# A mixture-of-experts kernel whose last block becomes a pair of experts, with a down projection in a half and two quarters of the columns

## The chip, the cores and the metric

One Trainium2 chip; the program runs on one core. The metric is the device time of one execution in microseconds (us). Three timed executions of the kernel before gave 731.32, 733.75 and 733.29 us, a median of 733.29.

## The reference

The input is 512 tokens of width 1024. One layer is computed: a mixer (two parallel groups of heads with a common input and output projection), then a mixture of experts, then a final RMSNorm. The change lies wholly in the mixture of experts and the norm:

```python
y = (silu(xb @ w1[e]) * (xb @ w3[e])) @ w2[e]      # one expert, 1024 -> 512 -> 1024, float32
out[token] += weight * y                            # two experts for each token
x = x + g2 * out
return x * rsqrt(mean(x * x) + 1e-6) * final_g
```

There are 32 experts; each has three matrices of 2 MB, so the experts' weights are some 200 MB, and each byte is read once.

## The kernel before, in words

The first part of the span (up to about 235 us) is the mixer, the router and the sorting of experts by the number of their tokens. The rest is 13 blocks (`BLOCKS`, line 30). A block takes 128 slots, which two experts share with 64 slots each (a pair) or four experts with 32 each (a quad). Ten blocks are pairs, three are quads. The order of the blocks is written out in line 30; the last one (number 12) is the quad `QUADS[2]`, and before it come four pairs.

**One block** (`block`, line 1075) does the following on TensorE, in an order written by hand (line 1280). `up` (line 1100) multiplies the gathered tokens by w1: eight steps of k, in each one product of 512 columns for each expert, and each product lies in its own strip of 32 or 64 of the array's columns. A SiLU goes to ScalarE, some small products and transposes follow (lines 1118 to 1125), then `up` with w3, the gating product on VectorE (line 1131), four transposes and a copy (`hidden_t`, line 971), and the down projection `mm` (line 1146): for each of four chunks q of the hidden width, for each half of the output columns, for each expert one product. In all blocks but the last, `expert_out` (line 979) then multiplies by the gate `g2b`, splits the result into a high and a low half (`split`, line 85: a copy on ScalarE, a subtraction on VectorE), and returns eight units of `combine_units` (line 955). A unit is two products that bring the 128 slots back to 128 tokens, for one half of the columns, and an addition to `x2` on VectorE. The units are run in the next block, between its other products; blocks 10 and 11 also gather the tokens of block 12.

**The last two blocks** differ. Block 12 has no tokens to gather for anyone, so `block` gets the eight units of block 11 as `along`, and runs one of them behind each of the eight steps of its w1 (line 1106). Ahead of it, once block 11 is done, lines 1301 to 1309 spread `final_g` over the partitions with copies on VectorE and products on TensorE.

**The weights** come by DMAs of the SP queue in the order in which the blocks need them (line 1093): w1, w3, w2 of a block, then the next block. They go through a ring of 12 buffers of 8 KB a partition (`RING`, line 38). One buffer is filled by two DMAs of 512 KB, one for each of two experts; a buffer is loaded again when TensorE has read it. The program gives eight semaphores in turn to the DMAs, so that a DMA is issued when the eighth one before it has landed. A row of a DMA is 4 KB long for w1, w3 and w2, except for the last block's w2, which is loaded by columns.

**The end.** `LAST` (line 42) cuts the last block's down projection into four parts of 256 columns, each with its own weights (rows of 1 KB). `y_part` (line 1320) runs the 16 products of a part (four chunks, four experts; the trace lists every such product twice), then the multiplication by `g2b` (line 1327) and, except in the last part, the split. `combine_part` (line 1337) brings a part back to the four groups of 128 tokens: products (line 1344), the addition on VectorE (line 1346), a sum of squares on ScalarE (line 1348); in the first two parts GpSimd multiplies by `fg` (line 1350). In the last part ScalarE also takes the square roots (line 1354). Lines 1371 to 1378 set the order: parts 0 and 1, combine 0, part 2, combine 1, part 3, combine 2, combine 3. In this stretch (line 1313) the order of every engine is the order of the program. `scales` and `finish` then scale the rows and send them out.

Of the kernel before, what the change touches and what calls it, by code (L numbers as in the profile page):

```python
# [12 lines left out]
OP = mybir.AluOpType  # L13
# [5 lines left out]
E, F, FC = 32, 512, 4  # L19
SLOT = 64  # L20
FIXED = 4
# [5 lines left out]

PAIRS = [(FIXED + 2 + i, 2) for i in range(0, MID, 2)]
QUADS = [(FIXED + 2 + MID + i, 4) for i in range(0, SMALL, 4)]
BLOCKS = [(0, 2), (2, 2), QUADS[0], PAIRS[0], (FIXED, 2), PAIRS[1], PAIRS[2], QUADS[1], *PAIRS[3:], QUADS[2]]  # L30
NB = len(BLOCKS)
FB, FA = 4, 3
F0 = 8
# [5 lines left out]
FIRST = ["wp"] * WP + ["wq"] * WQ + ["ft"] * 4 + ["l8"] * 3  # L39
WARM = 18  # L40
EPS = 1e-6
LAST = tuple((slice(c, c + 256), 4) for c in range(0, 1024, 256))


@with_exitstack
def trunk(ctx, tc, a, out):
    nc = tc.nc
    sync, act, pool, dve, pe = nc.sync, nc.scalar, nc.gpsimd, nc.vector, nc.tensor
# [15 lines left out]
    def bank(tag=None, shape=(P, 512), dt=F32):  # L64
        if tag is None:
            tag = ring[turn[0] % 3]
            turn[0] += 1
        return psum.tile(list(shape), dt, name=tag)
# [10 lines left out]
    def t2(shape):  # L79
        return ft.tile(list(shape), F32, name="t2", bufs=6)  # L80
# [98 lines left out]
    class Ada:  # L179
# [19 lines left out]
        def mm(self, kk=None):  # L199
            if kk != 1:  # L200
                self.ps = bank("m")
            for k in range(KD) if kk is None else range(4 * kk, 4 * kk + 4):
                j = k % 4
                pe.matmul(self.ps[32 * j:32 * j + 32], cond[:, k:k + 1].to_broadcast([P, 32]), self.w[k // 4][:, j, :],  # L204
                          start=(k < 4), stop=(k >= 4), tile_position=(0, 32 * j))
            if kk != 0:
                self.m = t2((P, 512))
                act.activation(self.m, self.ps, AF.Copy)
# [336 lines left out]
    for k in range(KD):  # L545
# [9 lines left out]
        if k == 4:  # L555
# [5 lines left out]
            for c in range(4):  # L561
                dve.scalar_tensor_tensor(sbb[:, c, :], pt[:, c, :], cb_("lnb", c), sbb[:, c, :], op0=OP.mult,
                                         op1=OP.add)
# [84 lines left out]
    for c in range(4):  # L648
# [3 lines left out]
        for t in range(NT):  # L652
            for h in range(2):
# [6 lines left out]
                                 op0=OP.mult, op1=OP.add)  # L660
# [369 lines left out]
    class Weights:  # L1030
# [3 lines left out]
        def __init__(self, name, b, f, cs=None, n=1):  # L1034
            if b not in experts:
                experts[b] = []
                for e in range(BLOCKS[b][0], BLOCKS[b][0] + BLOCKS[b][1]):
                    if e >= FIXED:
# [21 lines left out]
    def block_weights(b):  # L1060
        if b == NB - 1:
            w2 = [Weights("expert_w2", b, D, cs, n) for cs, n in LAST]
        else:
# [3 lines left out]
    def columns(b):  # L1067

        if BLOCKS[b][1] == 4:
            return [(32 * j, 32, j) for j in range(4)]  # L1070
        if BLOCKS[b][0] == FIXED:
            return [(32 * j, 32, j // 3) for j in range(4)]
        return [(64 * j, 64, j) for j in range(2)]

    def block(b, along, early, before_y, after):

        last = b == NB - 1
        p0, np_ = BLOCKS[b]
        cols = columns(b)
        w1, w3, w2 = block_weights(b) if b != 1 else second  # L1080
        if b == 0:
            slots.extend(FIRST)
            w3.load()
            w1.load(1)
            for w in w2:
                w.load()
            second.extend(block_weights(1))
            second[0].load(2)
            w1.load()
            xT4b.append(const.tile([P, KD, 4 * SLOT], F32, name="l8", bufs=5))  # L1090
            kept.append(const.tile([P, 2, D], F32R, name="l8", bufs=5))
        else:
            for w in [w1, w3] + w2:
                w.load()
        w1, w3, w2 = w1.r, w3.r, [w.r for w in w2]
        yb = kept[0]
        sl = slice((b % 2) * P, (b % 2 + 1) * P)
        g, xT = g4s[b // 2][:, :, sl], xT4b[b // 2 % 2][:, :, sl]

        def up(w, units=()):  # L1100
            h = bank("h")
            for k in range(KD):
                for c, n, j in cols:
                    pe.matmul(h[c:c + n], xT[:, k, c:c + n], w[j][k],  # L1104
                              start=(k == 0), stop=(k == KD - 1), tile_position=(0, c))
                for u in units[k:k + 1]:
                    u()
            return h

        if b == 0:  # L1110
            h3 = up(w3)
        h1 = up(w1, along)
        s = t2((P, F))
        act.activation(s, h1, AF.Silu)  # L1114
        if last:
            act.activation(over_i, s[:, 0:1], AF.Sqrt, scale=0.0, bias=eps)
        ps = bank("m", (P, 2, np_))
        for t in range(NT):
            pe.matmul(ps, g[:, t, :], wtp[:, t, :, p0:p0 + np_], start=(t == 0), stop=(t == NT - 1))  # L1119
        ws = small.tile([P, 9], F32, name="ws")  # L1120
        mine = of4 if np_ == 4 else of31 if p0 == FIXED else of2
        dve.scalar_tensor_tensor(ws[:, 0:2 * np_], ps.rearrange("p a b -> p (a b)"), 1.0,  # L1122
                                 mine.rearrange("p a b -> p (a b)"), op0=OP.mult, op1=OP.mult, accum_out=ws[:, 8:9])
        cT = ex.tile([P, NT, P], F32R, name="cT")
        transposed_onehot(g, cT)
        for u in early:
            u()
        if b > 0:
            h3 = up(w3)
        gt = t2((P, F))  # L1130
        dve.scalar_tensor_tensor(gt, s, ws[:, 8:9], h3, op0=OP.mult, op1=OP.mult)  # L1131
        if b == 0:
            over_count()
            second[0].load()
            second[1].load()
        for u in before_y:
            u()
        gT = hidden_t(gt)
        if b == 0:
            beyond(before_y)  # L1140
        if b > 0:
            for u in after:
                u()
        yh, yl = yb[:, 0], yb[:, 1]

        def mm(ys, i=None):
            for q in range(FC):
                for hf, y in enumerate(ys):
                    for c, n, j in cols:
                        w = w2[0][j][q][:, hf * F:(hf + 1) * F] if i is None else w2[i][j][q]  # L1150
                        pe.matmul(y[c:c + n], gT[:, q, c:c + n], w,  # L1151
                                  start=(q == 0), stop=(q == FC - 1), tile_position=(0, c))

        if last:
            return cT, mm
        expert_out(mm, yh, yl)
        if b == 0:
            for u in after:
                u()
        return combine_units(cT, yh, yl)  # L1160
# [93 lines left out]
    def onehots(b):  # L1254

        g = g4s[b // 2][:, :, (b % 2) * P:(b % 2 + 1) * P]
        p0, n = BLOCKS[b]
        if p0 == FIXED:
# [22 lines left out]
    for b in range(NB):  # L1281
        q = b // 2
# [31 lines left out]
    cT, mm = comb  # L1314
    o = out[0].rearrange("(t p) d -> p t d", p=P)
    fin = const.tile([P, len(LAST) + 4, NT], F32, name="fin")
    tags = ["c", "m", "c", "m", "h"]
    ncomb = [0]

    def y_part(i):  # L1320

        cs = LAST[i][0]
        n = cs.stop - cs.start
        y = bank("y", (P, n))
        mm([y], i)
        yf = t2((P, n))
        dve.tensor_tensor(yf, y, g2b[:, cs], op=OP.mult)
        if i == len(LAST) - 1:
            return ((cT.bitcast(F32), yf),)
        yh, yl = kept[0][:, 0, cs], kept[0][:, 1, cs]  # L1330
        split(yh, yl, yf)
        return (cT, yh), (cT, yl)

    n_parts = len(LAST)
    ms, base, both, v, r = [fin[:, n_parts - 1 + i] for i in range(5)]

    def combine_part(i, parts):
        cs = LAST[i][0]
        n = cs.stop - cs.start
        for t in range(NT):  # L1340
            ps = bank(tags[ncomb[0] % len(tags)], (P, n))
            ncomb[0] += 1
            for q, (w, y) in enumerate(parts):
                pe.matmul(ps, w[:, t, :], y, start=(q == 0), stop=(q == len(parts) - 1))
            xc = x2[:, t, cs]
            dve.tensor_tensor(xc, xc, ps, op=OP.add)
            sq = t2((P, n))
            act.activation(sq, xc, AF.Square, scale=1.0 / 32.0, accum_out=fin[:, i, t:t + 1])
            if i < n_parts - 2:
                pool.tensor_tensor(xc, xc, fg[:, cs], op=OP.mult)  # L1350
            tt = slice(t, t + 1)
            if i == n_parts - 1:
                dve.tensor_tensor(both[:, tt], base[:, tt], fin[:, i - 1, tt], op=OP.add)
                act.activation(r[:, tt], ms[:, tt], AF.Sqrt, bias=both[:, tt])
# [13 lines left out]
        for hf in (1, 0):  # L1368
            sync.dma_start(o[:, t, hf * 512:(hf + 1) * 512], x2[:, t, hf * 512:(hf + 1) * 512])

    todo = []
    for i in range(n_parts):
        todo.append((i, y_part(i)))
        if 0 < i < n_parts - 1:
            combine_part(*todo.pop(0))
    dve.scalar_tensor_tensor(base, fin[:, 0], EPS, fin[:, 1], op0=OP.add, op1=OP.add)
    for i, parts_ in todo:
        combine_part(i, parts_)
    for ts in (0, 1), (1, 3), (3, 4):
        scales(slice(*ts))  # L1380
        for t in range(*ts):
# [24 lines left out]
```

## Time and profile before

| | us |
|---|---|
| median of three timed executions | 733.29 |
| the profiled execution | 730.36 |
| its span (first to last instruction) | 728.6 |
| TensorE busy in it | 678.5 |
| VectorE busy | 295.6 |
| ScalarE busy | 174.8 |
| GpSimd busy | 24.4 |

The profiled execution is 1.76 us longer than its span, and 2.93 us (0.4%) shorter than the median. Times in the trace are microseconds from the start of the span. An engine's busy time is the union of its instructions; a wait is told by what ended it ("<-").

### The profile page before, as it was taken

What the parts mean: (1) busy time and instruction counts of PE and PEld (TensorE: products, weight loads), DVE (VectorE), ACT (ScalarE), POOL (GpSimd) and SP (SyncE); (2) the same over time, 40 slices, a digit from 0 to 9 for tenths busy, and PEclk for the clock granted to TensorE, in tenths of its full rate; (3) what the DMA queues carried; (4) which work ended last, traced back from release to release, by engine and by line L of the source; (5) the groups of instructions that cost most, each with busy time, mean ns of one, the idle gap of its engine ahead of it and who ended that gap; (6) DMA issues with size and microseconds to landing.
All of it is one profiled execution on the core that took longest, in us unless ns stands there. A gap on an engine that the chain in (4) does not pass through costs nothing.

```text
span 728.6 us, 10224 instructions
## 1 busy us (share of the span) xinstructions
PE 678.5 (93%) x3693; PEld 358.9 (49%) x3693; DVE 295.6 (41%) x690; ACT 174.8 (24%) x317; POOL 24.4 (3%) x55
## 2 busy tenths in 40 slices
PE   8799999999998999999999999989899999989873
PEld 6467766767887435432544444333144544442131
DVE  7459439452568823311333332221123322333025
ACT  5244496342344210100110110100001110111014
POOL 3000000000103000000000000000000000000011
PEclk9899999999999999999999999999999999999997
DMA  8999606885629869999999999999999999999993
GB/s 293 287 347 319 231 1 208 274 306 208 244 78 338 346 249 409 408 409 410 408 409 409 408 410 409 409 410 408 408 410 408 409 410 408 409 404 409 361 328 118
DMA packets 99487, 246.33 MB, mean 338 GB/s; under 512 B 14072, under 2 KB 40296, under 8 KB 99432
## 3 DMA queue, kind: packets, MB, share of 16 engines
q1 hardware_dynamic: 98152, 245.09, 88.6%
q8 instruction: 30, 0.49, 0.3%
q10 hardware_dynamic: 1056, 0.52, 0.3%
q14 instruction: 25, 0.20, 0.1%
q0 software_dynamic: 224, 0.02, 0.0%
HBM read 243.51 MB, written 2.10 MB: 337 GB/s over the span
## 4 chain that ended last, share of the span: by engine, by line
DMA 60%; PE 29%; DVE 4%; SPq 3%; ACT 3%; issue 1%; POOL 0%; DVEq 0%; ACTq 0%
DMA w8r<-in_expert_w 20%; DMA w<-in_expert_w 18%; DMA l<-in_expert_w 18%; PE h L1104 4%; PE c L437 3%; PE h L437 3%; PE y L1151 3%; PE y L437 2%; PE m L204 2%; DMA w<-in_ada_w 2%; SPq L260 1%; PE h L90 1%; PE h L91 1%; PE m L946 1%; PE h L92 1%; DMA sbb<-in_sgu_b 1%
## 5 line engine op out<-in xcount | busy, mean ns | idle before, releaser
L1104 PE MATMUL h<-w,l 128*64 128x512 f32 (+1 forms) x608 | 135.5, 598 | 5.1 <-DMA w<-in_expert_w 5.0
L961 DVE TENSOR_TENSOR x<-x,c 128x512 f32<-128x512 f32 x96 | 65.9, 686 | 39.4 <-PE c L960 39.4
L1104 PEld LDWEIGHTS h<-w,l 128*64 128x64 f32 (+1 forms) x608 | 37.1, 125 | 89.5 <-issue 56.6
L1104 PE MATMUL h<-w8r,l 128*32 128x512 f32 (+1 forms) x304 | 61.9, 598 | 2.8 <-DMA w8r<-in_expert_w 2.8
L960 PE MATMUL c<-l,cT 128*128 128x512 f32 x192 | 62.4, 406 | 0.0
L946 PE MATMUL m<-l,b16h 128*128 128x256 f32 (+1 forms) x192 | 51.8, 294 | 3.2 <-ACT l L817 3.1
L1151 PE MATMUL y<-w8q,gT 128*64 128x512 f32 (+2 forms) x240 | 50.0, 570 | 3.9 <-DMA w8q<-in_expert_w 2.3
L985 DVE TENSOR_TENSOR t<-y,g2b 128x512 f32<-128x512 f32 x24 | 16.6, 692 | 89.8 <-PE y L1151 88.5
L86 ACT ACTIVATE l<-t 128x512 fp32r<-128x512 f32 (+1 forms) x35 | 21.3, 613 | 130.3 <-DVE t L985 115.7
L1151 PE MATMUL y<-w8r,gT 128*64 128x512 f32 (+2 forms) x240 | 49.3, 566 | 3.2 <-DMA w8r<-in_expert_w 3.2
L1131 DVE SCALAR_TENSOR_TENSOR t<-t,ws,h 128x512 f32<-128x512 f32 x13 | 9.7, 747 | 98.6 <-PE h L1104 98.6
L946 PE MATMUL m<-l,b16l 128*128 128x256 f32 (+1 forms) x192 | 49.1, 279 | 0.0
L817 ACT ACTIVATE l<-m,s2c 128x256 f32<-128x256 f32 (+1 forms) x24 | 13.1, 547 | 147.6 <-PE m L946 147.6
L946 PEld LDWEIGHTS m<-l,b16h 128*128 128x128 f32 x192 | 36.1, 188 | 19.6 <-ACT l L817 8.3
L242 DVE TENSOR_TENSOR w8r<-w,w8r 128x512 fp32r<-128x512 f32 x48 | 30.7, 685 | 26.6 <-ACT w8r L240 26.6
L1104 PEld LDWEIGHTS h<-w8r,l 128*32 128x32 f32 (+1 forms) x304 | 16.3, 120 | 44.8 <-issue 26.0
L946 PEld LDWEIGHTS m<-l,b16l 128*128 128x128 f32 x192 | 36.3, 189 | 2.5
L240 ACT ACTIVATE w8r<-w 128x512 fp32r<-128x512 f32 x48 | 26.9, 621 | 33.5 <-PE h L92 17.6
L1122 DVE SCALAR_TENSOR_TENSOR ws<-m,of 128x4 f32<-128x4 f32 (+1 forms) x13 | 2.1, 163 | 80.1 <-PE m L1119 80.1
L437 PE MATMUL c<-b16h,w8r 128*128 128x512 f32 x80 | 31.2, 414 | 3.1 <-ACT b16h L406 2.6
L960 PEld LDWEIGHTS c<-l,cT 128*128 128x128 f32 x192 | 29.2, 189 | 6.7 <-issue 3.4
L1114 ACT ACTIVATE t<-h 128x512 f32<-128x512 f32 x13 | 7.8, 598 | 99.4 <-PE h L1104 99.4
(358 smaller groups left out, 953.8 us busy)
## 6 DMA issues: line engine op xcount, KB each, us to landing
w<-in_expert_w SPq DMA_DIRECT2D x160, 512.0 KB, 10.1
w8r<-in_expert_w SPq DMA_DIRECT2D x124, 512.0 KB, 10.2
w8q<-in_expert_w SPq DMA_DIRECT2D x64, 512.0 KB, 10.2
l<-in_expert_w SPq DMA_DIRECT2D x36, 512.0 KB, 10.3
w<-in_ada_w SPq DMA_DIRECT2D x32, 512.0 KB, 7.5
w<-in_w_in SPq DMA_DIRECT2D x8, 1024.0 KB, 8.9
w<-in_ada_w SPq DMA_DIRECT2D x8, 1024.0 KB, 11.1
w<-in_w_out SPq DMA_DIRECT2D x4, 1024.0 KB, 8.8
```

Source lines behind the costliest of these rows:

```text
L86: act.activation(hi, src, AF.Copy)
L204: pe.matmul(self.ps[32 * j:32 * j + 32], cond[:, k:k + 1].to_broadcast([P, 32]), self.w[k // 4][:, j, :], start=(k < 4), stop=(k >= 4), ti ...
L240: act.activation(hi, raw, AF.Copy)
L242: return lambda: dve.tensor_tensor(lo, raw, hi.bitcast(F32), op=OP.subtract)
L437: pe.matmul(ps[c], lhs, rhs, start=(k == 0 and n == 0), stop=(k == KD - 1 and n == 2))
L817: act.activation(o, ps, AF.Identity, scale=a2[:, k:k + 1], bias=sh2[:, k:k + 1])
L946: pe.matmul(hold[k], src[:, t, chunk(k)], g[:, t, :], start=(t == 0 and i == 0), stop=(t == NT - 1 and i == 1))
L960: pe.matmul(ps, cT[:, t, :], y[:, cs], start=(i == 0), stop=(i == 1))
L961: dve.tensor_tensor(x2[:, t, cs], x2[:, t, cs], ps, op=OP.add)
L985: dve.tensor_tensor(yf, y, g2b[:, cs], op=OP.mult)
L1104: pe.matmul(h[c:c + n], xT[:, k, c:c + n], w[j][k], start=(k == 0), stop=(k == KD - 1), tile_position=(0, c))
L1151: pe.matmul(y[c:c + n], gT[:, q, c:c + n], w, start=(q == 0), stop=(q == FC - 1), tile_position=(0, c))
```

## The change

The order of the last two blocks is exchanged: the quad becomes block 11, and the pair `PAIRS[6]` becomes block 12, the last. `LAST` cuts the last down projection into one part of 512 columns and two of 256; a second number says how many chunks q come in one DMA, now two. A part's weights are thus two buffers, of which the first holds chunks 0 and 1 of both experts and the second chunks 2 and 3. The rows of these DMAs are 2 KB in the first part and 1 KB in the others.

The products of parts 1 and 2 are cut after chunk 1, and in the cut the part before is combined. GpSimd's multiplication is now that of part 0 alone, which is as many columns as before. `base` is the sum of the first part alone; the sum of the second was already added in line 1353, as `fin[:, i - 1]`.

```diff
-BLOCKS = [(0, 2), (2, 2), QUADS[0], PAIRS[0], (FIXED, 2), PAIRS[1], PAIRS[2], QUADS[1], *PAIRS[3:], QUADS[2]]
+BLOCKS = [(0, 2), (2, 2), QUADS[0], PAIRS[0], (FIXED, 2), PAIRS[1], PAIRS[2], QUADS[1], *PAIRS[3:6], QUADS[2],
+          PAIRS[6]]
...
-LAST = tuple((slice(c, c + 256), 4) for c in range(0, 1024, 256))
+LAST = ((slice(0, 512), 2), (slice(512, 768), 2), (slice(768, 1024), 2))
...
-        def mm(ys, i=None):
-            for q in range(FC):
+        def mm(ys, i=None, qs=range(FC)):
+            for q in qs:
...
-    def y_part(i):
+    def y_part(i, between=None):
...
-        mm([y], i)
+        if between is None:
+            mm([y], i)
+        else:
+            mm([y], i, range(FC // 2))
+            between()
+            mm([y], i, range(FC // 2, FC))
...
-            if i < n_parts - 2:
+            if i == 0:
                 pool.tensor_tensor(xc, xc, fg[:, cs], op=OP.mult)
...
-    todo = []
-    for i in range(n_parts):
-        todo.append((i, y_part(i)))
-        if 0 < i < n_parts - 1:
-            combine_part(*todo.pop(0))
-    dve.scalar_tensor_tensor(base, fin[:, 0], EPS, fin[:, 1], op0=OP.add, op1=OP.add)
-    for i, parts_ in todo:
-        combine_part(i, parts_)
+    part0 = y_part(0)
+    part1 = y_part(1, lambda: combine_part(0, part0))
+
+    def second_part():
+        combine_part(1, part1)
+        dve.tensor_scalar(base, fin[:, 0], EPS, None, op0=OP.add)
+
+    combine_part(2, y_part(2, second_part))
```

## Rows read from the trace of the kernel before

**Rows 1.** The page's chain that ended last, share of the span by engine.
```profile
DMA 60%; PE 29%; DVE 4%; SPq 3%; ACT 3%; issue 1%; POOL 0%; DVEq 0%; ACTq 0%
```

**Rows 2.** Chain that ended last, from 690 us: start, duration, what.
```profile
691.84 8.48 DMA l<-in_expert_w
...
700.37 3.45 PE y L1151 x26
...
704.09 8.72 DMA w8r<-in_expert_w
...
712.85 1.93 PE y L1151 x26
...
714.80 0.42 DVE t L1327
...
715.29 1.69 DVE x L1346 x5
```

**Rows 3.** Stretches: length, busy PE, PEld, DVE, ACT, POOL; granted clock, DMA share, GB/s.
```profile
630.00:650.00 20.00, 19.97 (x108) 10.44 (x108) 6.81 (x11) 1.85 (x4) 0.00 (x0) 1.00 1.02 404
...
690.00:700.00 10.00, 5.54 (x48) 1.93 (x43) 1.60 (x3) 1.01 (x2) 0.00 (x0) 1.00 1.01 325
700.00:705.00 5.00, 4.63 (x36) 2.47 (x38) 0.67 (x2) 0.42 (x1) 0.00 (x0) 0.66 1.09 349
```

**Rows 4.** Timeline, end of the quad that is block 7 (start, us, engine, line, what).
```profile
523.06 1.90 PE L1151 MATMUL y<-w8r,gT 128*32 128x512 f32 x10 [0.22 <-DMA w8r<-in_expert_w]
```

**Rows 5.** Timeline, two pairs: half of a down projection, three quarters of w3.
```profile
582.47 3.65 PE L1151 MATMUL y<-w8q,gT 128*64 128x512 f32 x16
...
634.13 5.37 PE L1104 MATMUL h<-w,l 128*64 128x512 f32 x24
```

**Rows 6.** Timeline, TensorE from the end of block 11 to block 12's hidden width.
```profile
648.40 3.60 PE L1151 MATMUL y<-w8r,gT 128*64 128x512 f32 x16
...
655.80 1.07 PE L1104 MATMUL h<-w8r,l 128*32 128x512 f32 x8
...
662.44 1.92 PE L1104 MATMUL h<-w,l 128*32 128x512 f32 x8
...
670.08 0.62 PE L1104 MATMUL h<-w,l 128*32 128x512 f32 x2
...
672.48 2.56 PE L1104 MATMUL h<-w8q,l 128*32 128x512 f32 x15
...
689.10 1.90 PE L1104 MATMUL h<-w,l 128*32 128x512 f32 x10 [0.26 <-DMA w<-in_expert_w]
...
693.25 0.63 PE L1151 MATMUL y<-w,gT 128*32 128x256 f32 x6 [0.69 <-ACT gT L976]
```

**Rows 7.** Timeline, gate and split of block 11's 512 columns.
```profile
651.22 1.52 DVE L985 TENSOR_TENSOR t<-y,g2b 128x512 f32<-128x512 f32 x2 [5.58 <-PE y L1151]
...
652.67 0.69 DVE L87 TENSOR_TENSOR l<-t,l 128x512 fp32r<-128x512 f32 x1
```

**Rows 8.** Operations of 512 columns: page (busy, mean ns), and line 697 (ns).
```profile
L961 DVE TENSOR_TENSOR x<-x,c 128x512 f32<-128x512 f32 x96 | 65.9, 686 | 39.4 <-PE c L960 39.4
...
L697 ACT ACTIVATE b16l<-x x8: 615/624/632, 187.8 to 224.3; 128x512 fp32r<-128x512 f32 x8
```

**Rows 9.** Timeline, gate and split of part 0; its combination.
```profile
696.52 0.43 DVE L1327 TENSOR_TENSOR t<-y,g2b 128x256 f32<-128x256 f32 x1 [4.66 <-PE y L1151]
...
697.43 0.43 DVE L87 TENSOR_TENSOR l<-t,l 128x256 fp32r<-128x256 f32 x1 [0.48 <-ACT l L86]
...
703.74 0.51 PE L1344 MATMUL c<-l,cT 128*128 128x256 f32 x2
...
704.88 1.35 PE L1151 MATMUL y<-w8q,gT 128*32 128x256 f32 x6
...
706.14 2.79 POOL L1350 TENSOR_TENSOR x<-x,l 128x256 f32<-128x256 f32 x4 [480.37 <-ACT t L1348]
```

**Rows 10.** Timeline, the last combination: a product of TensorE, ScalarE's first square.
```profile
715.75 0.59 PE L1344 MATMUL c<-t,cT 128*128 128x256 f32 x2
...
717.37 0.40 ACT L1348 ACTIVATE t<-x 128x256 f32<-128x256 f32 x1
```

## The prediction

> **What bounds the kernel now.** I began with the chain by engine: DMA 60%, TensorE 29% [rows 1]. Read alone, this says that whatever makes the last weights land sooner is gained. The chain of the last 40 us shows how it does that [rows 2]: it alternates between DMAs of 8.5 to 8.7 us and short runs of products. The last weights land at 712.81, 1.93 us of products follow, then VectorE and ScalarE. The end is set from 717.37, where ScalarE takes the first square of the last part [rows 10]; from there it is busy with squares, roots and scaled rows until the end, and none of that work is changed. So I forecast the time of that square.
>
> Then the stretches, for the stream's speed [rows 3]: 404 GB/s with rows of 4 KB, 325 and 349 with the 1 KB rows of the last block. Last the timeline of TensorE, for a question that the chain doesn't answer: how far behind the stream is TensorE, and where? A quad's down projection waits for its last DMA and ends 1.90 us after it [rows 4]. In the last quad, too, the last products of w3 wait for their DMA, at 689.10 [rows 6]. A quad's products are no slower than a pair's, and a quad has twice the weights to wait for. The last block begins late (between the end of block 11's products, 652.00, and w1, 655.80, lie 3.80 us of `fg`), and it carries eight combination units; as a quad it has the time to make this up. The chain shows DMA at the end because the last block is a quad.
>
> **The change, part by part.**
>
> *The exchange.* In the old stream, 8 MiB of w2 lie behind the quad's last w3, which is there at 689.10. In the new one, 12 MiB lie behind the quad's last w2, so that this lands 4 MiB earlier: 4.19 MB at 408 GB/s (an estimate just above the 404 of rows 3) is 10.3 us, 678.8. TensorE ends the quad at 680.7 [rows 4], and the pair's w1 starts 3.8 us later, at 684.5, because the work for `fg` is the same.
>
> *The pair's w1 and w3.* A step of k with a combination unit takes 1.66 us ((662.44 - 655.80) / 4, rows 6), bare of waits. That was a quad's step, but a pair's costs the same (32 records of 0.224 us make 7.1 us for eight steps, rows 5, and eight records 1.07 us in rows 6). Seven steps are 11.6 us; from the start of the last step to w3 it is 2.4 us (670.08 to 672.48). So w3 starts at 698.5. It takes 7.1 us and ends at 705.7. The stream needs 8 MiB for w1 and w3, 20.6 us: the last w3 has landed at 699.4, over 6 us before it is used. The pair as last block is bound by TensorE, not by the stream. From the end of w3 to the first product of w2 it is 2.25 us (691.00 to 693.25): 707.9.
>
> *The weights of w2.* Their 4.19 MB take 10.3 us at 408 GB/s and 12.9 us at 325; the last land between 709.7 and 712.3, against 712.81 before. The twelve DMAs in the place of sixteen are issued without a new wait: the last two buffers of the ring are those of the pair's first w1, read by 691. I count the earlier landing at nothing, since the products that need the last DMA start only near 719 (below); that cover is some 7 us.
>
> First the row, then the rule: 1 KB rows land at 325 and 349 GB/s, 4 KB rows at 404 [rows 3]. The Trainium skill (Perfetto Trace Analysis, "DMA Optimizations") says that transfers under 2 KB pay overhead and that batching them into larger ones helps. The trace agrees on the rate; by that rule the change would gain 0.5 to 3.1 us, by the rows the gain is hidden.
>
> *The parts.* Each step of the new end, from 707.9 on, is on the path:
> 1. Part 0's eight products of 512 columns: 3.65 us [rows 5].
> 2. Gate, split, until the low half is there: from 651.22 to 653.36, 2.14, and some 0.06 to start a product: 2.2 us [rows 7].
> 3. Combine 0: some 0.4 us for the first product and 2.5 for four additions. One of 512 columns takes 0.69 [rows 8]; five of 256 take 1.69 [rows 2], 0.34 each where one lasts 0.41, so I take some 0.61 a piece. Together 2.9 us. Behind these additions stands the gate of part 1 on VectorE's queue.
> 4. Part 1's gate and split: 696.52 to 697.86, 1.34 us [rows 9], and 0.3 more because its copy stands behind the square of 512 columns (0.62, rows 8) on ScalarE: 1.65 us. Part 1's second four products stand behind combine 0 on TensorE, but end before VectorE is free.
> 5. Combine 1: 703.74 to 704.88 for its eight products, 1.0 us once the low half is there [rows 9].
> 6. Part 2's second four products stand behind combine 1: 1.0 us (a quarter of rows 5's eight, 0.9, and the drain).
> 7. Gate 0.43, the first exact product 0.59 [rows 10], starts: 1.1 us; addition and start of the square: 0.45 us.
>
> The sum is 13.95 us: the first square starts at 721.9, **4.5 us later** than at 717.37.
>
> What goes: combine 2 no longer stands behind the last products, and ScalarE's four old squares not ahead of the first new one; both are in the sum already, since it compares squares. GpSimd's multiplication grows from 0.70 us (four in 2.79) to at most 1.4 a row group, 5.6 us in all [rows 9]; it begins near 716 and ends near 722, ahead of ScalarE's scaled rows. There are seven gates and splits (three of them of 512 columns) where there were ten of 256; what falls away lay beside the path.
>
> **The sum.** 730.36 + 4.5 = 734.9 us for the profiled execution. The median of the runs is 2.93 us above it, so I put the prediction at 737.8. Bounds: a w1 step of 1.2 us instead of 1.66 would take 3.2 us off; a landing of the quad's weights 0.6 us later (a rate of 385 GB/s over the 4 MiB less) adds 0.6; the estimates in steps 3 to 7 may be off by 1.5 us both ways. The forecast's own range is 735.5 to 740.
>
> **The rivals.**
>
> *The stream decides (faster).* If TensorE reached the end of w3 with the stream, the last landing, 710.2 (0.5 us above the early bound), would be followed by three products (0.65 us and a start), gate, exact product, addition: the first square would start at 712.8, 4.6 us earlier than now, 728.7. For it: the chain [rows 1, 2], and that this is what happens in the quad. Against it: at 684.5 two of the pair's four w1 buffers have landed, and TensorE has 21 us of products and units to do for what the stream brings in 20.6, of which 5.7 have passed. It decides if the start of w1 moves forward by more than 6 us. I give it 0.11.
>
> *Part of the lag vanishes (near no change).* If the pair's steps, two strips wide, overlap with the units as a quad's do not, w1 takes 9.6 us rather than 13.3; the delay becomes 0.8 to 1.3 us, 734.1 to 734.6. For it: some TensorE records overlap. Against it: the pitch is the sum of both in rows 6. 0.13.
>
> *The clock falls in the new end (slower still).* From 700.37 the same 26 records take 3.45 us that take 1.93 at 712.85 [rows 2], and the granted clock of 700 to 705 is 0.66 [rows 3]: part of it at 1.2 instead of 2.4 GHz. Before this, TensorE was busy for 5.54 of 10 us, waiting between parts. The new end has such waits too (steps 2 to 4). If it falls there, the products of steps 3, 5, 6 and 7 on the path, some 2.5 us, double: 7 us of delay, 740.3. 0.14. [...]
>
> *It doesn't do what it says.* "Combined amid the next products" is to hide the combination under the wait for weights. When the weights are already there, the cut hides nothing and only makes the second half of the products wait: this is the forecast itself, not another time.
>
> **How the numbers follow.** The forecast has 0.62, the rivals 0.11, 0.13 and 0.14. A difference of 0.3%, 2.2 us, is about what a measurement of this kernel can tell from no change. Slower: nearly all of the forecast, the clock, a fifth of the partial lag: 0.79. Same: the rest of the partial lag and a little of the two neighbours, 0.12. Faster: most of the first rival, 0.09. The range goes from 733.8, which takes in the partial lag, to 741.0, with most of the clock's case; some 0.11 lies below and 0.06 above.
>
> **What would show it.** Right: the pair's w1 starts some 5.7 us after the quad's last weights; w3 runs without a wait for DMA, in one piece of 7.1 us; the products of part 0 find their weights landed; TensorE's waits in the last 15 us are for VectorE and ScalarE; the first square of the last part starts near 721.9, and the chain of the end names gates, splits and additions, not DMA. Wrong: waits for DMA in w3 or between the parts, a last landing followed by the end within 16 us, or a w1 whose steps with units are much shorter than 1.66 us.

## The result and the profile after

The median of eight runs is 738.42 us (736.20 to 741.77), against 733.33 us for eight runs of the kernel before: **slower** by 0.8%, ratio 1.0082, 95% interval 1.006 to 1.0105. The profiled execution took 738.84 us.

The page's head and its chain by engine, to be held against [rows 1]:

```profile
span 736.7 us, 10104 instructions
...
DMA 55%; PE 33%; DVE 5%; ACT 3%; SPq 2%; issue 1%; POOL 0%; DVEq 0%; ACTq 0%
```

DMA loses 5 points of the chain and TensorE gains 4. Where they change hands stands in the chain that ended last, from 671 us (start, duration, what), the counterpart of [rows 2]:

```profile
671.51 10.21 DMA w8r<-in_expert_w
...
681.77 1.92 PE y L1152 x10
...
701.63 7.04 PE h L1105 x32
...
710.91 3.68 PE y L1152 x16
...
717.28 1.90 DVE x L1352 x3
...
722.13 1.41 DVE x L1352 x4
723.54 0.52 DVE fin L1382
```

The last DMA of the chain ends at 681.72, with the quad's last weights. Before, the last DMA of the chain ended at 712.81 [rows 2]. From 681.77 on the chain has no wait for weights: the gate and the work for `fg`, up products, down products, gates, additions. Whether the stream was late at all is read from stretches (length, busy PE, PEld, DVE, ACT, POOL; granted clock, DMA share, GB/s), as in [rows 3]:

```profile
684.00:701.00 17.00, 15.52 (x68) 6.28 (x68) 8.54 (x15) 1.55 (x4) 0.00 (x0) 1.00 1.03 402
701.00:711.00 10.00, 8.39 (x45) 3.21 (x46) 1.45 (x4) 2.60 (x4) 0.00 (x0) 1.00 0.84 281
711.00:716.00 5.00, 4.43 (x24) 1.54 (x24) 0.69 (x2) 0.63 (x1) 0.00 (x0) 1.00 0.03 11
716.00:726.00 10.00, 8.32 (x47) 5.45 (x48) 7.31 (x17) 4.89 (x18) 5.18 (x4) 1.00 0.00 0
```

The stream is all but over at 711 (11 GB/s over the next 5 us, then 0), just when the first down product starts. The granted clock is 1.00 in all four stretches, that is 2.4 GHz.

Last the timeline of the new end (start, duration, engine, line, operation; in brackets what ended an idle time), which answers to [rows 4, 6, 7, 9, 10]:

```profile
681.77 1.90 PE L1152 MATMUL y<-w8r,gT 128*32 128x512 f32 x10 [0.24 <-DMA w8r<-in_expert_w]
...
687.43 1.08 PE L1105 MATMUL h<-w8r,l 128*64 128x512 f32 x4
...
689.10 1.08 PE L1105 MATMUL h<-w8r,l 128*64 128x512 f32 x4
...
701.56 4.94 PE L1105 MATMUL h<-w,l 128*64 128x512 f32 x22
...
710.91 3.65 PE L1152 MATMUL y<-w8q,gT 128*64 128x512 f32 x16 [0.69 <-ACT gT L977]
...
716.02 0.50 PE L1350 MATMUL c<-l,cT 128*128 128x512 f32 x1 [0.59 <-ACT l L87]
...
716.74 0.50 PE L1350 MATMUL c<-l,cT 128*128 128x512 f32 x1 [0.22 <-DVE l L88]
...
718.86 5.18 POOL L1356 TENSOR_TENSOR x<-x,l 128x512 f32<-128x512 f32 x4 [489.98 <-ACT t L1354]
...
719.69 0.42 DVE L1333 TENSOR_TENSOR t<-y,g2b 128x256 f32<-128x256 f32 x1
...
720.95 0.70 DVE L88 TENSOR_TENSOR l<-t,l 128x256 fp32r<-128x256 f32 x1 [0.83 <-ACT l L87]
721.70 0.39 PE L1350 MATMUL h<-l,cT 128*128 128x256 f32 x1 [0.35 <-DVE l L88]
...
722.73 1.08 PE L1152 MATMUL y<-w8r,gT 128*64 128x256 f32 x8
...
723.46 0.60 DVE L1382 TENSOR_SCALAR fin<-fin 128x4 f32<-128x4 f32 x1
...
725.68 0.42 ACT L1354 ACTIVATE t<-x 128x256 f32<-128x256 f32 x1 [1.34 <-issue]
```

The first square of the last part starts at 725.68 instead of 717.37, 8.3 us later. Not all of that is the change. Three quarters of block 10's w3, work that the change leaves alone, stand in the timelines of before and of after like this:

```profile
602.73 5.37 PE L1104 MATMUL h<-w,l 128*64 128x512 f32 x24
```

```profile
605.84 5.37 PE L1105 MATMUL h<-w,l 128*64 128x512 f32 x24
```

So 3.1 us had gone by earlier in this one execution, and 5.2 us are the change's; the medians say 5.1. The 3.1 us were already there before the blocks: an up product of the first of them starts at 243.49 before and at 246.59 after. In what follows each run's first square is therefore taken from its own start of this group: 114.64 us in before (717.37 - 602.73), 119.84 in after.

### The profile page after: what moved, and what is told of

Its sections match the earlier page's. It is cut to its first block, busy times and chain, and to the rows that moved or that the text cites. A ratio compares the mean times of both kernels' runs of the same rounds, so it can differ in the third digit from the quotient of the medians.

```text
span 736.7 us, 10104 instructions
## 1 busy us (share of the span) xinstructions
PE 686.3 (93%) x3637; PEld 357.6 (49%) x3637; DVE 296.1 (40%) x684; ACT 173.8 (24%) x308; POOL 24.0 (3%) x51
## 4 chain that ended last, share of the span: by engine, by line
DMA 55%; PE 33%; DVE 5%; ACT 3%; SPq 2%; issue 1%; POOL 0%; DVEq 0%; ACTq 0%
DMA w8r<-in_expert_w 18%; DMA w<-in_expert_w 17%; DMA l<-in_expert_w 17%; PE h L1105 6%; PE c L438 4%; PE h L438 3%; PE y L1152 3%; PE m L205 2%; PE y L438 2%; DMA w<-in_ada_w 2%; SPq L261 2%; PE h L91 1%; PE h L92 1%; PE m L947 1%; PE h L93 1%; PE c L961 1%
## 5 line engine op out<-in xcount | busy, mean ns | idle before, releaser
L1105 PE MATMUL h<-w,l 128*64 128x512 f32 (+1 forms) x608 | 139.9, 598 | 6.4 <-DMA w<-in_expert_w 6.1
L1152 PE MATMUL y<-w8q,gT 128*64 128x512 f32 (+1 forms) x224 | 51.9, 599 | 4.4 <-DMA w8q<-in_expert_w 2.1
L1152 PE MATMUL y<-w8r,gT 128*64 128x512 f32 (+2 forms) x240 | 51.6, 567 | 2.2 <-DMA w8r<-in_expert_w 2.1
```

Of the source, the lines that this page charges most:

```text
L1105: pe.matmul(h[c:c + n], xT[:, k, c:c + n], w[j][k], start=(k == 0), stop=(k == KD - 1), tile_position=(0, c))
L1152: pe.matmul(y[c:c + n], gT[:, q, c:c + n], w, start=(q == 0), stop=(q == FC - 1), tile_position=(0, c))
```

## The experiments

The theory after the result: with a pair at the end TensorE, not the stream, sets the end, and the pair's combination units, the work for `fg` and the cut products all stand in line. The rivals: the new parts cost in themselves; the last weights still land late; the clock falls. Seven kernels ran. The first four each undo one part of the change or take away its load.

**The exchange alone**: after's order of blocks, before's four quarters.

```diff
-BLOCKS = [..., *PAIRS[3:], QUADS[2]]
+BLOCKS = [..., *PAIRS[3:6], QUADS[2], PAIRS[6]]
```

> The pair is the last block, but with the four old parts of 256 columns, each run whole, and the old order. Theory (TensorE is late in a last pair, and the cut costs time on top): w1 still starts 5.7 us after the quad's last weights and w3 never waits for a DMA; from the first down product to the last part's first square it is about 11.8 us instead of 14.8, since a part's gate and split lie beside the next part's products. So 3.0 us faster than the changed kernel, 2.1 us slower than the kernel before: ratio about 1.003. Rival (the loss comes from the new parts alone, and a last pair is bound by the stream): as fast as before or up to 2 us faster, ratio 0.997 to 1.000.

Measured: 735.97 us, ratio 1.005 (1.0028 to 1.0072). From its timeline:

```profile
710.23 3.67 PE L1152 MATMUL y<-w8q,gT 128*64 128x256 f32 x32 [0.69 <-ACT gT L977]
...
723.15 0.40 ACT L1349 ACTIVATE t<-x 128x256 f32<-128x256 f32 x1
```

Both quarters of the first group run as one piece of 3.67 us, with no wait for a DMA between them: the weights are there. The first square is 12.9 us behind the first down product, 118.0 us on the common scale, 3.4 us later than before. So most of the loss is the exchange's, and the other 1.8 us come with the new parts and their cut. The theory had expected less: 11.8 us from the first down product to the square, and 2.1 us against before. Its ratio of 1.003 lies in the interval, the rival's doesn't.

**The parts alone**: after's three parts and its cut, before's order of blocks.

```diff
-BLOCKS = [..., *PAIRS[3:6], QUADS[2], PAIRS[6]]
+BLOCKS = [..., *PAIRS[3:], QUADS[2]]
```

> The quad stays the last block; the half, the two quarters and the cut are applied to it (its weights come in eight DMAs of 512 KB with rows of 2 KB, then sixteen of 256 KB with rows of 1 KB). Theory: in a last quad the stream decides, so the cut does what it is meant to do there: the last landing comes 1.4 us earlier and five products stand behind it instead of thirteen; combine 1 is done by then. The last part's first square comes some 3.5 us earlier than in the kernel before: ratio about 0.995. Rival (the cut and the new parts are what costs, wherever they stand): slower than before, ratio 1.003 or more.

Measured: 729.81 us, ratio 0.9971 (0.9954 to 0.9988), **faster than both kernels**, though by no more than the 0.3% that the prediction took as about the least that can be told. The first square is at 111.8 on the common scale, 2.9 us earlier than before; 3.5 us and a ratio of 0.995 were expected. Its chain that ended last:

```profile
705.22 5.72 DMA w8r<-in_expert_w
...
710.98 1.05 PE y L1151 x10
...
713.17 1.59 PE y L1151 x16
```

```profile
716.50 0.42 ACT L1353 ACTIVATE t<-x 128x256 f32<-128x256 f32 x1 [1.77 <-issue]
```

Here DMA is in the chain until 710.94. The same parts and the same cut that go with a loss behind the pair go with a gain behind the quad. So the first rival, that the parts cost wherever they stand, falls. Behind the pair they do cost: 1.8 us, by the run before this one.

**Without the pair's units**: `fill` isn't passed to the last block, so eight combination units of block 11 and their 16 products are gone.

```diff
         if b == NB - 1:
-            comb = block(b, fill, [], [], [])
+            comb = block(b, [], [], [], [])
```

> The changed kernel without the eight combination units of block 11, which stand between the steps of the last pair's w1 (block 11's share of the output is left out). Theory: w1 takes 7 us instead of 13.4, w3 waits for DMAs again and ends near their last landing, and the end comes about 5 us earlier than in the changed kernel: level with the kernel before, ratio 0.999 to 1.002. Rival (TensorE's place against the stream doesn't matter, the end is a chain of the new parts or of their DMAs): as slow as the changed kernel, ratio about 1.007.

Measured: 733.26 us, ratio 1.002 (1.0003 to 1.0038). From its timeline:

```profile
679.57 1.90 PE L1152 MATMUL y<-w8r,gT 128*32 128x512 f32 x10 [0.23 <-DMA w8r<-in_expert_w]
...
685.23 3.65 PE L1105 MATMUL h<-w8r,l 128*64 128x512 f32 x16
...
693.18 6.21 PE L1105 MATMUL h<-w,l 128*64 128x512 f32 x24
...
700.71 1.93 PE L1105 MATMUL h<-l,l 128*64 128x512 f32 x6 [0.21 <-DMA l<-in_expert_w]
...
704.88 3.65 PE L1152 MATMUL y<-w8q,gT 128*64 128x512 f32 x16 [0.69 <-ACT gT L977]
...
719.66 0.42 ACT L1354 ACTIVATE t<-x 128x256 f32<-128x256 f32 x1 [1.33 <-issue]
```

w1 now takes 7.95 us (685.23 to 693.18) where it took 14.1, 6.2 less. But w3 now waits for DMAs: from its start to its end (702.64) it takes 9.46 us instead of 7.04. Relief of 6.2 us on TensorE brings the first down product only 3.8 us nearer to the quad's last weights (25.3 us behind them instead of 29.1), and then the stream decides when w3 ends. So the border that the prediction put at "more than 6 us" lies near 3.8: it compared the last landing with the end of w3, but six records of products, 1.93 us, still stand behind that landing.

Nor does the stream decide the end of this kernel. The first square is 14.8 us behind the first down product, as in after, and none of the products between them waits for a DMA. The ratio is at the upper end of what was expected, 0.999 to 1.002.

**No cut**: the same parts in the order part 0, part 1, combine 0, part 2, combine 1, combine 2, so that each gate has products beside it.

```diff
-    part1 = y_part(1, lambda: combine_part(0, part0))
-    def second_part():
-        combine_part(1, part1)
-        dve.tensor_scalar(base, fin[:, 0], EPS, None, op0=OP.add)
-    combine_part(2, y_part(2, second_part))
+    part1 = y_part(1)
+    combine_part(0, part0)
+    part2 = y_part(2)
+    combine_part(1, part1)
+    dve.tensor_scalar(base, fin[:, 0], EPS, None, op0=OP.add)
+    combine_part(2, part2)
```

> The changed kernel with its half and two quarters, but every part's products run whole: part 0, part 1, combine 0, part 2, combine 1, combine 2. Theory: with the weights already there the cut only makes products wait for gates and splits; without it part 1's products cover part 0's gate and split, and the last part's first square comes about 2.7 us earlier than in the changed kernel: 2.4 us slower than before, ratio about 1.003. Rival (the cut is free, all of the loss is TensorE's lateness): as the changed kernel, ratio about 1.007. Second rival (the cut saves time, as it is meant to): slower than the changed kernel, above 1.009.

Measured: 736.02 us, ratio 1.0063 (1.0035 to 1.009). By the ratio alone this is rather the first rival's case (about 1.007) than the theory's (about 1.003), and the interval overlaps with after's; what the cut costs is read from the timeline:

```profile
709.55 3.66 PE L1152 MATMUL y<-w8q,gT 128*64 128x512 f32 x16 [0.69 <-ACT gT L977]
...
718.02 5.00 POOL L1356 TENSOR_TENSOR x<-x,l 128x512 f32<-128x512 f32 x4 [489.63 <-ACT t L1354]
...
720.97 0.85 DVE L1382 TENSOR_SCALAR fin<-fin 128x4 f32<-128x4 f32 x1
...
722.07 0.97 DVE L1359 TENSOR_TENSOR fin<-fin 128x1 f32<-128x1 f32 x1
722.24 0.42 ACT L1354 ACTIVATE t<-x 128x256 f32<-128x256 f32 x1 [0.39 <-DVE x L1352]
```

The first square is 12.7 us behind the first down product, not 14.8: behind the pair the cut costs 2.1 us. But some 0.8 us come back behind it: two tiny operations of VectorE, 128x4 and 128x1 numbers, take 0.85 and 0.97 us. One of 128x4 takes 0.15 in before (line 1376), one of 128x1 takes 0.15 elsewhere in this run. Both fall into GpSimd's 5.00 us. That called for the last but one experiment below.

**The final gain later**: the copies and the 16 products for `fg` move out of the gap between blocks 11 and 12; the first half stands ahead of part 0's products, the second amid part 1's.

```diff
-        if b == NB - 2:
...
-                for q in range(4):
-                    pe.matmul(ps[:, q * P:(q + 1) * P], gain[:, q, :], ident, start=True, stop=True)
-                dve.tensor_scalar(fg[:, hf * 512:(hf + 1) * 512], ps, -0.5, None, op0=OP.mult)
...
+    def gains(hf):
+        spread_.append(bank("h"))
+        for q in range(4):
+            pe.matmul(spread_[hf][:, q * P:(q + 1) * P], gain[hf][:, q, :], ident, start=True, stop=True)
+    def gained(hf):
+        dve.tensor_scalar(fg[:, hf * 512:(hf + 1) * 512], spread_[hf], -0.5, None, op0=OP.mult)
+    gains(0)
+    gained(0)
     part0 = y_part(0)
-    part1 = y_part(1, lambda: combine_part(0, part0))
+    def first_part():
+        gains(1)
+        combine_part(0, part0)
+    part1 = y_part(1, first_part)
...
-    combine_part(2, y_part(2, second_part))
+    part2 = y_part(2, second_part)
+    gained(1)
+    combine_part(2, part2)
```

> The kernel after with the final gain's copies and 128x128 products moved out of the gap between blocks 11 and 12: the first half stands just ahead of part 0's products (in the wait for the gates), the second half amid part 1's. Theory (nothing hides the gap of 3.74 us between the quad's last down product, 683.69, and the pair's first up product, 687.43, because the stream is far ahead by then): 2.7 to 3.7 us of it vanish, the pair's w1 starts about 1 us after the quad's end or at once, and the time falls by 2.5 to 3.5 us from the kernel after's: ratio to the kernel before 1.0035 to 1.005, near 735.5 to 736. Rival (the gap only covers a wait for the last weights or for the pair's own inputs): a wait for a DMA appears in the pair's w1 or w3 or in part 0's products, and the time stays within 1 us of the kernel after's, ratio 1.007 to 1.009.

Measured: 734.80 us, ratio 1.005 (1.0031 to 1.007). From its timeline:

```profile
679.48 1.90 PE L1152 MATMUL y<-w8r,gT 128*32 128x512 f32 x10 [0.24 <-DMA w8r<-in_expert_w]
681.31 1.79 PE L1105 MATMUL h<-w8r,l 128*64 128x512 f32 x4
...
696.15 5.37 PE L1105 MATMUL h<-w,l 128*64 128x512 f32 x24
...
705.64 3.65 PE L1152 MATMUL y<-w8q,gT 128*64 128x512 f32 x16
...
720.42 0.42 ACT L1345 ACTIVATE t<-x 128x256 f32<-128x256 f32 x1 [1.34 <-issue]
```

The pair's w1 starts at the quad's end, at 681.31, without the gap of 3.74 us; its first group takes 0.7 us more, and still nothing before part 0's products waits for a DMA. On the common scale the first square comes at 116.85, 3.0 us earlier than in after. The theory's figure held; the rival's wait for weights did not come.

**Without GpSimd's multiplication**: to see what slowed VectorE.

```diff
-            if i == 0:
-                pool.tensor_tensor(xc, xc, fg[:, cs], op=OP.mult)
```

> The kernel after without GpSimd's four multiplications of the first half by the final gain: the output lacks that gain in its first 512 columns. Theory (VectorE's work on SBUF alone runs slower while GpSimd multiplies): the 128x256 subtraction L88 of part 1 takes 0.43 us again instead of 0.70 and the sum ahead of the base 0.15 instead of 0.60, so that part 2's first square comes 0.3 to 0.7 us earlier after the first down product (14.77 us now, 14.1 to 14.5 then); ratio to the kernel before 1.0072 less 0.0005 to 0.001, that is 1.006 to 1.008. Rival (these times come from the order on VectorE or from waits on PSUM, not from GpSimd): both durations stay at 0.70 and 0.60 and the first square at 14.8 us after.

Measured: 737.07 us, ratio 1.0064 (1.0042 to 1.0087). The two operations of VectorE:

```profile
720.65 0.42 DVE L88 TENSOR_TENSOR l<-t,l 128x256 fp32r<-128x256 f32 x1 [0.83 <-ACT l L87]
...
722.89 0.16 DVE L1380 TENSOR_SCALAR fin<-fin 128x4 f32<-128x4 f32 x1
...
725.00 0.42 ACT L1354 ACTIVATE t<-x 128x256 f32<-128x256 f32 x1 [1.22 <-issue]
```

0.42 and 0.16 us in the place of 0.70 and 0.60. The first down product is at 710.60, the first square at 725.00, 14.4 us behind it instead of 14.8. The cause is GpSimd, and it costs 0.4 us in this kernel; the ratios alone would not show so little.

**The quad last, no cut**: the second kernel's order of blocks with the fourth's order of parts.

> The old order of blocks (the quad last) with the half and two quarters, each combined after the whole of the next part's products, not amid them. If the cut costs in itself (two waits for gates stand on TensorE, 0.5 us ahead of part 2's combine in the run with the cut): part 2's first square comes 0.5 to 1 us earlier than with the cut (716.50 at a front that was 2.0 us later than before's), of which VectorE gives back up to 0.5 while GpSimd multiplies: ratio to the kernel before 0.9955 to 0.997. If the last landing sets the end instead, part 2's products wait for a DMA and the ratio is that of the run with the cut, 0.997 or 0.998.

Measured: 729.90 us, ratio 0.9965 (0.9949 to 0.9981), not to be told from the run with the cut (0.9971). Its chain:

```profile
708.29 5.59 DMA w<-in_expert_w
...
713.92 1.06 PE y L1151 x10
```

```profile
717.61 0.42 ACT L1353 ACTIVATE t<-x 128x256 f32<-128x256 f32 x1
```

The chain stays on DMA until 713.87. With the cut it left DMA at 710.94, and what followed ended no later. So behind the quad the last landing and the line on TensorE are close together, and the cut neither costs nor gives anything that these runs can tell: on the common scale the square is 0.85 us later than with the cut, while the ratio is 0.0006 lower. The ratio alone lies in the range of the first expectation, but the earlier square that this asked for did not come; the second (the stream sets the end) is what the chain shows.

## Why the prediction was right

The forecast was 737.8 us, 4.5 more than before; the median is 738.42, 5.1 more. Each step of the forecast beside what after's trace shows; the trace's early part is 3.1 us later throughout. Less these 3.1 us the quad's last weights are there at 678.7, where 678.8 was forecast.

| Step | Forecast | Measured |
|---|---|---|
| quad's last weights to w1's start | 5.7 us | 5.66 (681.77 to 687.43) |
| pitch of a w1 step with a unit | 1.66 | 1.67 |
| w1's start to w3's start | 14.0 | 14.1 |
| w3, no wait for a DMA | 7.1 | 7.04 |
| w3's end to the first down product | 2.25 | 2.2 |
| 1, part 0 | 3.65 | 3.7 |
| 2, gate and split to the low half | 2.2 | 2.1 |
| 3, combine 0 | 2.9 | 2.95 |
| 4, part 1's gate and split | 1.65 | 2.0 |
| 5, combine 1 | 1.0 | 1.0 |
| 6, part 2's second half | 1.0 | 1.1 |
| 7, to the first square | 1.55 | 1.9 |
| first down product to first square | 13.95 | 14.8 |

- **The lag is right.** The prediction looked past the chain's 60% of DMA to where TensorE stands against the stream, and dated the new line from the quad's last landing. Every step up to the first down product is within 0.15 us. The run without units shows why the stream's rival had to fail, and that it was mis-sized twice. It takes 3.8 us of relief on TensorE, not more than 6, before w3 meets the stream. And the end would not have come three products behind the last landing: in that run the line of the parts still stands behind w3, and the first square is 1.4 us later than before, not 4.6 earlier.
- **The mis-sized terms are steps 4 and 7**, 0.35 and 0.3 us too short. The prediction let GpSimd's 5.6 us lie beside the path because ScalarE's scaled rows come later. It did. But VectorE's subtraction L88 and the sum L1382 fall into the same time and took 0.70 and 0.60 us for 0.43 and 0.15. Without GpSimd's work they took 0.42 and 0.16. That makes nearly 0.3 us in step 4 and 0.1 in step 7. The rest of step 4 is ScalarE's copy, which started 0.4 us behind the gate's end (forecast: 0.3); the rest of step 7 is the first exact product, 0.70 us for the forecast's 0.59, and the starts. With all of it the change is 5.2 us, not 4.5.
- **"It doesn't do what it says" as the forecast itself held.** The cut hides nothing behind the pair: removing it brings the first square 2.1 us nearer to the first down product. Behind the quad, where weights are late, it costs nothing that can be told.
- **The vanishing lag fell** with the pitch: 1.67 us, strips and units in line. **The clock's rival fell** too: TensorE's waits of steps 2 to 4 came, the longest of 0.59 us (at 716.02), and the granted clock stayed at 1.00 until 726.
- **What the prediction did not say**: the change is two edits with opposite signs. The parts alone gain 0.29%, the exchange alone loses 0.5%, and together they lose 0.82%, more than the sum. What the parts gain lies in good part at the stream, which the exchange takes out of the chain: on the common scale of the table below the last wait for weights ends at 110.1 us in before (712.85 - 602.73) and at 108.9 with the quad last and no cut (713.92 - 604.98), and from there to the first square it is 4.5 us in the one (712.85 to 717.37) and 3.7 in the other (713.92 to 717.61). So 1.2 us come from an earlier landing and 0.8 from a shorter end. Why the landing is earlier stays open. With the quad last and no cut the stream carries 387 GB/s from 690 to 695, where the half's 2 KB rows come (before, with 1 KB rows, 297), but 240 from 700 to 705, where the quarters' smaller DMAs come (before 349). The weights of the first 512 columns are complete no earlier than before (97.5 on the common scale, before 97.6). No run tells rows, sizes and order apart.

The whole set on the common scale (from block 10's w3 to the first square of the last part), beside the ratios:

| Kernel | w3 of block 10 | First square | Between them, us | Against before | Ratio |
|---|---|---|---|---|---|
| before | 602.73 | 717.37 | 114.64 | | |
| after | 605.84 | 725.68 | 119.84 | +5.2 | 1.0082 |
| exchange alone | 605.12 | 723.15 | 118.03 | +3.4 | 1.005 |
| parts alone | 604.72 | 716.50 | 111.78 | -2.9 | 0.9971 |
| without units | 603.62 | 719.66 | 116.04 | +1.4 | 1.002 |
| no cut | 604.91 | 722.24 | 117.33 | +2.7 | 1.0063 |
| gain later | 603.57 | 720.42 | 116.85 | +2.2 | 1.005 |
| without GpSimd's work | 605.53 | 725.00 | 119.47 | +4.8 | 1.0064 |
| quad last, no cut | 604.98 | 717.61 | 112.63 | -2.0 | 0.9965 |

The signs agree throughout, and most sizes within 1 us (0.1% of a ratio is 0.73 us). The two that differ most are no cut (2.7 us here, 4.6 by its ratio) and gain later (2.2 and 3.7); the first lies in its ratio's interval, the second just below its edge. 0.8 us of the first are VectorE's stalls behind the square; the rest stays open. The scale itself is good to some 0.8 us: in the run without a cut, block 9's w3 and block 10's are 30.4 us apart, in the others 31.2.

## What to carry to other kernels

A chain with 60% of DMA says that the stream sets the end of this order of work, not of another: before a block is moved to the end, date its first product from the landing ahead of it and count what stands in line behind. To cut a product in two and put other work between can pay only where the second half waits for data; behind the quad, where it does, no gain showed that these runs can tell. Where the data are there, whole products beside each gate are better, here by 2.1 us. And test the halves of a change by themselves: here one half alone was the better kernel.

## What the runs showed of the hardware

GpSimd's work on SBUF holds up VectorE, but only some of its instructions. In after, L1382 starts at 723.46 and ends at 724.06; GpSimd's four multiplications end at 724.04 (718.86 + 5.18). In the run without a cut the 128x1 sum ends at 723.04, GpSimd at 723.02. So these two tiny operations were held until GpSimd's instruction was done, however little they had to do. The additions out of PSUM in the same stretch were not: 0.68 us for one of 512 columns with and without GpSimd.

The Trainium skill (SBUF — State Buffer, "Who interferes with whom") says that a VectorE instruction with two inputs in SBUF contends with a GpSimd instruction that reads SBUF, and that one with at most one such input, outside VectorE's two-port modes, doesn't. The trace agrees, with 0.70 us against 0.42 for L88's two SBUF inputs of 128x256 and 0.97 against 0.15 for two of 128x1. The same section names `tensor_scalar` among the operations that can enter a two-port mode and then contend. L1382 is one, and it took 0.60 us against 0.16; which mode it ran in, no run here shows.
